# One row of low and high parts: products of 256, 272 and 264 columns, with the sample sums joined after the product

## The chip, the core and the metric

The kernel runs on one core of one Trainium2 chip. The metric is the device time of one execution in microseconds (us). Three runs of the kernel before gave 1385.54 to 1386.02 us, with a median of 1385.92 us. The core has a matrix engine (PE, with its weight loads listed as PEld), a vector engine (DVE), a scalar engine (ACT), a third elementwise engine (POOL) and a queue for transfers (SP). Each works through its own instructions in their written order and waits for the others by semaphores.

## The reference

One layer of a hybrid decoder is computed in float32, for a prompt of 256 tokens and for 8 samples of one token each. D is 2048. Cut to the products:

```
x, w_in ... : float32
xn = rms_norm(x, g_mix)
z  = xn @ w_in                       # 2048 -> 3584
u_pool, u_lru, u_gel, c_a, c_b = split(z)
y_pool = pool_mixer(u_pool) @ w_pool_br          # 512 -> 2048
y_lru  = (rg_lru(conv4(u_lru)) * gelu(u_gel)) @ w_lru_br     # 1024 -> 2048
y_conf = silu(layer_norm(conv31(c_a * sigmoid(c_b)))) @ w_conf_br
g_a, g_b, g_c = split(sigmoid(xn @ w_gate + b_gate))         # 2048 -> 6144
x = x + (g_a * y_pool + g_b * y_lru + g_c * y_conf) @ w_out
hid = square(relu(rms_norm(x, g_mlp) @ w_up))                # 2048 -> 8192
x = x + hid @ w_down                                         # 8192 -> 2048
y = rms_norm(x, g_final)
```

Both token groups go through the same weights, so the kernel puts them side by side: 256 prompt columns and 8 sample columns, N = 264 columns in all. The samples also carry small states (convolution tails, the recurrence's last value) that are read and written back.

## The kernel before

**Three products for one.** Float32 accuracy is reached with products of the type float32r. Each weight w is split into a high part `whi` (w rounded to float32r, a cast on ACT, line 190) and a low part `wlo = w - whi` (a subtraction on DVE, line 191). Each activation is split in the same way into a high and a low part. One 128x128 block of weights then takes three products into the same accumulator `acc` of 128x264: whi by high (line 207), whi by low (line 208), wlo by high (line 209). The small fourth product, wlo by low, is left out. In the first four chunks line 920 issues the same products in another order. A weight block is loaded anew for each product.

**Chunks and groups.** Weights arrive in chunks of 128x1024 values (two rows of four 128x128 blocks). A group is a stretch of 512 output columns: four accumulators, filled over 8 chunks for an inner size of 2048, 4 for 1024 and 2 for 512. There are 67 dense groups. The 8 gate blocks of the recurrence and the pooling's group map are four half-size chunks and one more. The main loop walks over the chunks; for chunk i it issues the cast and the subtraction of chunk i+3, then the products of chunk i, at the end of a group the evacuation of its four accumulators, and then background work (`run_bg`): the convolutions, the scan, the norms, given out by credits for each engine and by delays in chunks (`later`).

**What sets the order.** Every engine follows this one written order. Four buffers hold split weights (`NHI = 4`), so the cast of chunk i+3 waits for the last product of chunk i-1. There are 8 accumulators: four for the group that runs, four for the one being emptied. The two parts of an activation lie in tiles at a pitch of 320 columns, high parts first and low parts behind them: `A` (the normalised input, later the merged branches and the hidden values), `L` and `LH` (the recurrence), `Q` (pooling and Conformer branch), `xn2` (the MLP's input).

**Places that the prediction speaks of.** `branch_evac` at line 769 multiplies an accumulator of a branch by its gate on DVE; for the Conformer branch POOL adds the other branches (line 775), and one and two chunks later ACT and DVE split the sum into `A` (lines 781 and 785). `down_evac` (line 855) adds an accumulator to the residual X; in the last quarter of the MLP it is followed by a square on ACT (line 818), an addition on POOL (line 820) and a scaling on ACT (line 860). The last two chunks of the kernel are interleaved by accumulator, so that the four accumulators of the last group are done one after the other. `last_evac` (lines 849 and 850) empties the very last one in two halves. A product with `ones` (line 1013) then sums the squares, ACT takes the root (line 1020), DVE refines it (lines 1025 to 1027), and the scaled rows are sent out (lines 1036 and 1037).

Of the kernel before, what the change touches and what calls it, by code (L numbers as in the profile page):

```python
# [15 lines left out]
P = 128  # L16
D = 2048
TP = 256
TS = 8
# [27 lines left out]
PITCH = 320  # L47
# [43 lines left out]
def hybrid_step(ctx: ExitStack, tc: tile.TileContext, first, par_in, st_in, wall, y_out, st_out):  # L91
# [14 lines left out]
    a_all = cpool.tile([P, 32 * PITCH], F32R, name="A")  # L106
    b_all = [cpool.tile([P, 8 * PITCH], F32, name=f"tmp{i}", tag=f"B{i}") for i in range(4)]
    qtmp = cpool.tile([P, 16 * PITCH], F32, name="qtmp", tag="Q")
    L = cpool.tile([P, 16 * PITCH], F32R, name="L", tag="L")
# [14 lines left out]
    def operand(t, k):  # L124
        return t[:, k * PITCH:k * PITCH + N]

    def operands(t, k, n=2):
        return t[:, k * PITCH:(k + n) * PITCH].rearrange("p (k c) -> p k c", k=n)[:, :, :N]

    def A(k):  # L130
        return operand(a_all, k)

    def acc():
        return psum.tile([P, 512], F32, name="acc", tag="acc")

# [70 lines left out]
    def mm3(ps, whi_t, wlo_t, xh, xl, first, last):  # L206
        nc.tensor.matmul(ps[:, :N], whi_t, xh, start=first, stop=False)  # L207
        nc.tensor.matmul(ps[:, :N], whi_t, xl, start=False, stop=False)  # L208
        nc.tensor.matmul(ps[:, :N], wlo_t, xh, start=False, stop=last)  # L209
# [138 lines left out]
    def x_sum():  # L348
        nc.vector.tensor_tensor(sq4[:, 0:2, :], sq4[:, 0:2, :], sq4[:, 2:4, :], op=ALU.add)
        nc.vector.tensor_tensor(sq4[:, 0, :], sq4[:, 0, :], sq4[:, 1, :], op=ALU.add)  # L350
        spend(dve=1.2)
        later(1, lambda: total_fold(operand(L, 0), G[:, 10, :], sq4[:, 0, :]))

    def x_rms():
        rms_close(operand(L, 0))
        later(1, lru_x_scale)
# [44 lines left out]
    def LH(s):  # L401
        if not l_at:
            l_at.append(cpool.tile([P, 16 * PITCH], F32R, name="LH", tag="L"))
        return operands(l_at[0], s.start) if isinstance(s, slice) else operand(l_at[0], s)
# [66 lines left out]
    def lru_gate_mm(ct, c, j):  # L471
# [9 lines left out]
        nc.scalar.activation(TM[:, ct, :], out[1][:, :N], AF.Sigmoid, bias=pv("b_lru_x", ct))  # L481
# [9 lines left out]
    def lru_tail():  # L491
# [3 lines left out]
        def scratch():  # L495
            S.append(operands(cpool.tile([P, 16 * PITCH], F32, name="lscr", tag="L"), 0, 8))
# [93 lines left out]
    def conf():  # L590
# [33 lines left out]
        def mean():  # L624
            kept.append(ones_mm(Q(4)))

        def halves():
            total_fold(Q(4), CT[:, 1, :], CT[:, 0, :])
# [42 lines left out]
        stage_split(q, 2, lambda c: Q(slice(4 + 2 * c, 6 + 2 * c)), lambda c: Q(slice(12 + 2 * c, 14 + 2 * c)),  # L671
# [15 lines left out]
    def Q(s):  # L687
        if not q_at:
            q_at.append(cpool.tile([P, 16 * PITCH], F32R, name="Q", tag="Q"))
        return operands(q_at[0], s.start) if isinstance(s, slice) else operand(q_at[0], s)  # L690

    def pooling():
# [28 lines left out]
        stage_split("pool", 2, lambda c: Q(slice(2 * c, 2 * c + 2)), lambda c: Q(slice(8 + 2 * c, 10 + 2 * c)), lambda c: DU[:, 2 * c:2 * c + 2, :])  # L721
        mark("pool", "pool")

    def grp_mm(c):
        assert "pool" in done
        hi, lo = whi[:, c % NHI, :], wlo[:, c % NHI, :]
        for gi in range(4):
            s = slice(gi * P, (gi + 1) * P)
            ps = acc()
            mm3(ps, hi[:, s], lo[:, s], Q(gi), Q(8 + gi), True, True)  # L730
            nc.scalar.activation(DU[:, gi, :], ps[:, :N], AF.Copy, scale=pv("pool_scale", gi))
        stage_split("pool", 2, lambda c: Q(slice(2 * c, 2 * c + 2)), lambda c: Q(slice(8 + 2 * c, 10 + 2 * c)), lambda c: DU[:, 2 * c:2 * c + 2, :])
# [5 lines left out]
    def bpart(k):  # L738
        if not M:
            M.extend(cpool.tile([P, 8 * PITCH], F32R, name=f"xn2{i}", tag=f"B{i}") for i in range(4))  # L740
        return operand(M[k // 8], k % 8), operand(M[2 + k // 8], k % 8)
# [52 lines left out]
    def out_evac(m, ps):  # L794
# [3 lines left out]
        hi, lo = bpart(m)  # L798
# [13 lines left out]
        if m == KD - 1:  # L812
            later(4, lambda: total_fold(LH(0), G[:, 10, :], sq2))
            later(6, lambda: rms_close(LH(0)))
# [7 lines left out]
    def hid(q, k):  # L822
        if q % 2 == 0:
            return A(k), A(16 + k)
        return LH(k), Q(k)

    def up_evac(q, m, ps):
        hi, lo = hid(q, m)
# [23 lines left out]
    def down_evac(q, m, ps):  # L852
        if (q, m) == (3, KD - 1):
            return last_evac(ps)
# [10 lines left out]
    def group(gi):  # L865
        name, k0, _, m = groups[gi]
        if name == "w_in":
            def rhs(i):
                return A(i), A(16 + i)
# [3 lines left out]
        if name == "w_gate":  # L873
            return (lambda i: (A(i), A(16 + i))), (lambda c, p: gate_evac(m // 4, m % 4, c, p))
        if name == "w_pool_br":
            assert "grp" in done
            return (lambda i: (Q(i), Q(8 + i))), (lambda c, p: branch_evac(0, m, c, p))
        if name == "w_lru_br":
            assert "lru" in done
            return (lambda i: (LH(i), LH(8 + i))), (lambda c, p: branch_evac(1, m, c, p))  # L880
        if name == "w_conf_br":
            assert "conf" in done
            return (lambda i: (Q(4 + i), Q(12 + i))), (lambda c, p: branch_evac(2, m, c, p))
        if name == "w_out":
            return (lambda i: (A(i), A(16 + i))), (lambda c, p: out_evac(m * 4 + c, p))
        if name == "w_up":
            return bpart, (lambda c, p: up_evac(m // 4, (m % 4) * 4 + c, p))
        q = k0 // 16
        return (lambda i: hid(q, i)), (lambda c, p: down_evac(q, m * 4 + c, p))
# [260 lines left out]
```

## Time and profile before

| | us |
|---|---|
| three runs: median, lowest, highest | 1385.92, 1385.54, 1386.02 |
| the profiled execution | 1385.61 |
| its span, first to last instruction | 1383.8 |
| PE busy | 1373.5 |
| DVE busy | 835.4 |
| ACT busy | 721.5 |
| POOL busy | 94.4 |

The page of a profile gives each engine's busy time, its busy tenths in 40 slices of the span, the transfers, the chain of work that ended last, and the costliest groups of instructions. A row such as `L209 PE MATMUL acc<-A,wlo 128*128 128x264 f32 x1952` is a group: line, engine, operation, the tiles written and read, the shape and the count. In a timeline each row has a start, a length, and in brackets how long the engine had been idle before it and what ended that. The length of a product includes its way through the pipeline and overlaps the next product; how long a product really takes from the engine is read from the distance between two starts.

### The profile page before, as it was taken

What the parts mean: (1) busy time and instruction counts of PE and PEld (TensorE: products, weight loads), DVE (VectorE), ACT (ScalarE), POOL (GpSimd) and SP (SyncE); (2) the same over time, 40 slices, a digit from 0 to 9 for tenths busy, and PEclk for the clock granted to TensorE, in tenths of its full rate; (3) what the DMA queues carried; (4) which work ended last, traced back from release to release, by engine and by line L of the source; (5) the groups of instructions that cost most, each with busy time, mean ns of one, the idle gap of its engine ahead of it and who ended that gap; (6) DMA issues with size and microseconds to landing.
All of it is one profiled execution on the core that took longest, in us unless ns stands there. A gap on an engine that the chain in (4) does not pass through costs nothing.

```text
span 1383.8 us, 26656 instructions
## 1 busy us (share of the span) xinstructions
PE 1373.5 (99%) x11421; PEld 1371.8 (99%) x11421; DVE 835.4 (60%) x1052; ACT 721.5 (52%) x1021; POOL 94.4 (7%) x125
## 2 busy tenths in 40 slices
PE   9999999999999999999999999999999999999997
PEld 9999999999999999999999999999999999999997
DVE  8785787776766658565555455555455545455544
ACT  7757576666664645455544334543344533354544
POOL 0220010110102013010000000000000000000012
PEclk9999999999999999999999999999999999999999
DMA  8555555555565554655555555555555555555552
GB/s 331 205 177 190 187 189 189 182 185 183 183 216 181 180 184 158 209 179 178 194 182 184 183 183 184 184 184 184 182 184 184 183 184 184 184 185 182 184 182 76
DMA packets 40822, 257.49 MB, mean 186 GB/s; under 512 B 4480, under 2 KB 6784, under 8 KB 11776
## 3 DMA queue, kind: packets, MB, share of 16 engines
q1 hardware_dynamic: 40272, 255.19, 53.3%
q8 instruction: 89, 1.46, 0.4%
q10 hardware_dynamic: 432, 0.61, 0.1%
q14 instruction: 29, 0.24, 0.1%
HBM read 252.57 MB, written 3.21 MB: 185 GB/s over the span
## 4 chain that ended last, share of the span: by engine, by line
PE 99%; DVE 0%; DVEq 0%; ACT 0%; issue 0%
PE acc L209 33%; PE acc L208 33%; PE acc L207 32%; PE acc L920 1%; PE acc L301 0%; DVE y L1036 0%; DVE acc L1027 0%; DVEq L1127 0%; DVE G L1026 0%; DVE acc L1025 0%; PE acc L1013 0%; PE acc L284 0%; ACT rstd L1020 0%; DVE G L850 0%; DVE X L849 0%
## 5 line engine op out<-in xcount | busy, mean ns | idle before, releaser
L191 DVE TENSOR_TENSOR wlo<-raw,whi 128x1024 fp32r<-128x1024 f32 (+1 forms) x478 | 585.0, 1226 | 523.8 <-ACT whi L190 523.4
L190 ACT CAST whi<-raw 128x1024 fp32r<-128x1024 f32 (+1 forms) x478 | 494.7, 1038 | 595.2 <-PE acc L208 546.1
L209 PE MATMUL acc<-A,wlo 128*128 128x264 f32 x1952 | 553.1, 283 | 0.0
L208 PE MATMUL acc<-A,whi 128*128 128x264 f32 x1952 | 552.4, 283 | 0.0
L207 PE MATMUL acc<-A,whi 128*128 128x264 f32 x1952 | 546.9, 280 | 0.0
L207 PEld LDWEIGHTS acc<-A,whi 128*128 128x128 f32 x1952 | 366.8, 188 | 0.0
L209 PEld LDWEIGHTS acc<-A,wlo 128*128 128x128 f32 x1952 | 365.9, 187 | 0.0
L208 PEld LDWEIGHTS acc<-A,whi 128*128 128x128 f32 x1952 | 365.7, 187 | 0.0
L209 PE MATMUL acc<-xn,wlo 128*128 128x264 f32 x1024 | 291.7, 285 | 0.0
L207 PE MATMUL acc<-xn,whi 128*128 128x264 f32 x1024 | 289.2, 282 | 0.0
L208 PE MATMUL acc<-xn,whi 128*128 128x264 f32 x1024 | 286.0, 279 | 0.0
L208 PEld LDWEIGHTS acc<-xn,whi 128*128 128x128 f32 x1024 | 192.5, 188 | 0.0
L207 PEld LDWEIGHTS acc<-xn,whi 128*128 128x128 f32 x1024 | 192.2, 188 | 0.0
L209 PEld LDWEIGHTS acc<-xn,wlo 128*128 128x128 f32 x1024 | 191.5, 187 | 0.0
L209 PE MATMUL acc<-LH,wlo 128*128 128x264 f32 x640 | 182.1, 285 | 0.0
L208 PE MATMUL acc<-Q,whi 128*128 128x264 f32 x644 | 180.5, 280 | 0.0
L207 PE MATMUL acc<-LH,whi 128*128 128x264 f32 x640 | 180.4, 282 | 0.0
L208 PEld LDWEIGHTS acc<-Q,whi 128*128 128x128 f32 x644 | 120.9, 188 | 0.0
L207 PEld LDWEIGHTS acc<-LH,whi 128*128 128x128 f32 x640 | 120.2, 188 | 0.0
L209 PEld LDWEIGHTS acc<-LH,wlo 128*128 128x128 f32 x640 | 119.8, 187 | 0.0
L820 POOL TENSOR_TENSOR G<-G 128x264 f32<-128x264 f32 x28 | 25.7, 919 | 796.8 <-ACT G L818 795.9
L600 ACT ACTIVATE G<-tmp,par 128x256 f32<-128x256 f32 x120 | 54.2, 499 | 1.5 <-DVE G L603 0.8
(194 smaller groups left out, 791.0 us busy)
## 6 DMA issues: line engine op xcount, KB each, us to landing
raw<-wall_dram SPq DMA_DIRECT2D x226, 1024.0 KB, 4.8
raw<-wall_dram SPq DMA_DIRECT2D x12, 512.0 KB, 6.1
raw<-first_dram SPq DMA_DIRECT2D x6, 512.0 KB, 8.3
X<-first_dram SPq DMA_DIRECT2D x6, 264.0 KB, 7.8
raw<-wall_dram SPq DMA_DIRECT2D x5, 256.0 KB, 3.0
tmp<-first_dram SPq DMA_DIRECT2D x3, 388.0 KB, 4.8
y_dram<-y SPq DMA_DIRECT2D x3, 264.0 KB, 2.2
tmp<-st_dram SPq DMA_DIRECT2D x4, 188.0 KB, 5.2
```

Of the source, the lines that this page charges most:

```text
L190: nc.scalar.copy(h[:, s], r[:, s])
L191: nc.vector.tensor_tensor(lo[:, s], r[:, s], f(h[:, s]), op=ALU.subtract)
L207: nc.tensor.matmul(ps[:, :N], whi_t, xh, start=first, stop=False)
L208: nc.tensor.matmul(ps[:, :N], whi_t, xl, start=False, stop=False)
L209: nc.tensor.matmul(ps[:, :N], wlo_t, xh, start=False, stop=last)
L600: nc.scalar.activation(dst[:, ct, :TP], vext[:, ct, k:k + TP], AF.Copy, scale=par[:, w:w + 1])
L820: nc.gpsimd.tensor_tensor(sq2, sq2, t, op=ALU.add)
L920: nc.tensor.matmul(pss[m][:, :N], w[:, i % NHI, s], x, start=i == kt == k == 0, stop=False)
```

## The change

The low and the high part of an activation now lie in one row of 528 columns: 264 low columns (256 prompt, 8 sample) and then 264 high columns (256 prompt, 8 sample). The pitch is 640, and the row begins 56 columns in. The three products are cut in another way:

- whi by columns 0 to 255 of the row: the low parts of the prompt, 256 columns, into columns 8 to 263 of the accumulator
- whi by columns 256 to 527: the low parts of the samples and all high parts, 272 columns, into columns 0 to 271
- wlo by columns 264 to 527: all high parts, 264 columns, into columns 8 to 271

So the accumulator has the low part of the sample sums in columns 0 to 7, the prompt in columns 8 to 263 and the rest of the sample sums in columns 264 to 271. `join` adds the two: ACT copies columns 0 to 7 to a small tile `side`, and DVE adds that to columns 264 to 271. It runs once for each of the 288 accumulators, ahead of the evacuation, which then reads columns 8 to 271 (`tokens`). In the first triple of an accumulator the product of 272 columns goes first, since it starts the sum; elsewhere the order is 256, 272, 264. The number of products and of weight loads is unchanged.

```diff
-PITCH = 320
+PITCH = 640
+SKEW = 56
...
-    a_all = cpool.tile([P, 32 * PITCH], F32R, name="A")
-    b_all = [cpool.tile([P, 8 * PITCH], F32, name=f"tmp{i}", tag=f"B{i}") for i in range(4)]
+    a_all = cpool.tile([P, KD * PITCH], F32R, name="A")
+    b_all = [cpool.tile([P, 4 * PITCH], F32, name=f"tmp{i}", tag=f"B{i}") for i in range(4)]
...
+    def part(t, k, a, n):
+        at = k * PITCH + SKEW + a
+        return t[:, at:at + n]
...
+    def both(t, k):
+        return part(t, k, 0, 2 * N)
...
+    def tokens(ps):
+        return ps[:, TS:TS + N]
+
+    side, joined = cpool.tile([P, 4, TS], F32, name="side"), []
+
+    def join(ps):
+        t = side[:, len(joined) % 4, :]
+        joined.append(t)
+        nc.scalar.copy(t, ps[:, :TS])
+        nc.vector.tensor_tensor(ps[:, N:N + TS], ps[:, N:N + TS], t, op=ALU.add)
...
-    def mm3(ps, whi_t, wlo_t, xh, xl, first, last):
-        nc.tensor.matmul(ps[:, :N], whi_t, xh, start=first, stop=False)
-        nc.tensor.matmul(ps[:, :N], whi_t, xl, start=False, stop=False)
-        nc.tensor.matmul(ps[:, :N], wlo_t, xh, start=False, stop=last)
+    def mm(k, ps, w, x, start, stop=False):
+        a, b = ((TP, 2 * N), (0, TP), (N, 2 * N))[k]
+        o = (0, TS, TS)[k]
+        nc.tensor.matmul(ps[:, o:o + b - a], w, x[:, a:b], start=start, stop=stop, skip_group_check=True)
+
+    def mm3(ps, whi_t, wlo_t, x, first, last):
+        for k in (0, 1) if first else (1, 0):
+            mm(k, ps, whi_t, x, first and k == 0)
+        mm(2, ps, wlo_t, x, False, last)
...
-            mm3(ps, hi[:, s], lo[:, s], operand(L, ct), operand(L, 8 + ct), True, True)
+            mm3(ps, hi[:, s], lo[:, s], both(L, ct), True, True)
+            join(ps)
             out.append(ps)
-        nc.scalar.activation(RA[:, ct, :], out[0][:, :N], AF.Sigmoid, bias=pv("b_lru_a", ct))
+        nc.scalar.activation(RA[:, ct, :], tokens(out[0]), AF.Sigmoid, bias=pv("b_lru_a", ct))
...
-    def last_evac(ps):
+    def last_evac(whole):
         m = KD - 1
         for s in (slice(0, N // 2), slice(N // 2, N)):
+            if s.start:
+                join(whole)
+            ps = tokens(whole)
             x = X[:, m, s]
             nc.vector.tensor_tensor(x, x, ps[:, s], op=ALU.add)
...
                 for m in range(4):
-                    fn(m, pss[m])
+                    if (gi, m) == (len(groups) - 1, 3):
+                        last_evac(pss[m])
+                    else:
+                        join(pss[m])
+                        fn(m, tokens(pss[m]))
```

The other edits fetch the parts from their new places (`high`, `low`, `highs`, `lows` in place of `operand` and `operands`).

In the change, lines stand some 30 to 40 further down: the products are on line 237, the cast and the subtraction on 218 and 219, the copy and the addition of `join` on 161 and 162, the square and the scaling of the tail on 854 and 897, the additions of the residual on 892 and 888. On PE, in the second group of the kernel, where the last accumulator's first triple is followed by the first accumulator's second one, the change now has:

```order
L237 MATMUL acc<-A,whi 128x272
L237 MATMUL acc<-A,whi 128x256
L237 MATMUL acc<-A,wlo 128x264
L237 MATMUL acc<-A,whi 128x256
L237 MATMUL acc<-A,whi 128x272
L237 MATMUL acc<-A,wlo 128x264
```

Nothing moved on PE but the widths and, after the first triple, the order of the low and the high product.

On DVE the Conformer branch's groups of two chunks each (subtraction `wlo` of two chunks, four evacuations, four low parts of `A`) stood before as

```order
L191 TENSOR_TENSOR wlo<-raw,whi 128x1024 x2
L769 TENSOR_TENSOR G<-acc,G 128x264 x4
L785 TENSOR_TENSOR A<-G,A 128x264 x4
L191 TENSOR_TENSOR wlo<-raw,whi 128x1024 x2
L769 TENSOR_TENSOR G<-acc,G 128x264 x4
```

and stand in the change as

```order
L219 TENSOR_TENSOR wlo<-raw,whi 128x1024 x2
L162 TENSOR_TENSOR acc<-acc,side 128x8
L805 TENSOR_TENSOR G<-acc,G 128x264
L162 TENSOR_TENSOR acc<-acc,side 128x8
L805 TENSOR_TENSOR G<-acc,G 128x264
L162 TENSOR_TENSOR acc<-acc,side 128x8
L805 TENSOR_TENSOR G<-acc,G 128x264
L162 TENSOR_TENSOR acc<-acc,side 128x8
L805 TENSOR_TENSOR G<-acc,G 128x264
L821 TENSOR_TENSOR A<-G,A 128x264 x4
```

Ahead of each evacuation stands the addition of `join`, which waits for ACT's copy.

On ACT the end of the program, from the last casts of weights to the roots, was before

```order
L190 CAST whi<-raw 128x1024 x3
L990 ACT_TABLE_LOAD
L818 ACTIVATE G<-X 128x264
L860 ACTIVATE X<-X,gfin 128x264
L818 ACTIVATE G<-X 128x264
L860 ACTIVATE X<-X,gfin 128x264
L818 ACTIVATE G<-X 128x264
L860 ACTIVATE X<-X,gfin 128x264
L1020 ACTIVATE rstd<-acc,eps 128x132 x2
```

and is in the change

```order
L218 CAST whi<-raw 128x1024 x3
L1030 ACT_TABLE_LOAD
L161 COPY side<-acc 128x8 x4
L854 ACTIVATE G<-X 128x264
L897 ACTIVATE X<-X,gfin 128x264
L854 ACTIVATE G<-X 128x264
L897 ACTIVATE X<-X,gfin 128x264
L854 ACTIVATE G<-X 128x264
L897 ACTIVATE X<-X,gfin 128x264
L1060 ACTIVATE rstd<-acc,eps 128x132 x2
```

The copies for all four accumulators of the last group, the very last one among them, now stand ahead of the squares and scalings of the first three.

More of the change, by code (lines that the diff above doesn't have):

```diff
@@ L399, in hybrid_step, with LH @@
     l_at = []
[L401 removed]
+    def LH():
         if not l_at:
[L403 to L404 removed]
+            l_at.append(cpool.tile([P, 8 * PITCH], F32R, name="LH", tag="L"))
+        return l_at[0]
     def two(c):
@@ L685, in hybrid_step, with Q @@
     q_at = []
-    def Q(s):
+    def Q():
         if not q_at:
-            q_at.append(cpool.tile([P, 16 * PITCH], F32R, name="Q", tag="Q"))
-        return operands(q_at[0], s.start) if isinstance(s, slice) else operand(q_at[0], s)
+            q_at.append(cpool.tile([P, 8 * PITCH], F32R, name="Q", tag="Q"))
+        return q_at[0]
     def pooling():
```

93 lines of the change are left out of this document (49 added, 44 removed).

## The prediction

> **What bounds the kernel now.** I read the page first, for the engine that carries the span and for the chain of work that ended last.
>
> ```profile
> span 1383.8 us, 26656 instructions
> PE 1373.5 (99%) x11421; PEld 1371.8 (99%) x11421; DVE 835.4 (60%) x1052; ACT 721.5 (52%) x1021; POOL 94.4 (7%) x125
> ...
> PE   9999999999999999999999999999999999999997
> ...
> PE 99%; DVE 0%; DVEq 0%; ACT 0%; issue 0%
> ```
>
> PE is busy in every slice, and the chain is PE from end to end. Next comes the view of who waited for whom, for PE alone:
>
> ```profile
> PE acc L301 <- PEq L1121: 0.8, 1, 0.8
> PE acc L1013 <- DVE G L850: 0.3, 1, 0.3
> ```
>
> PE never waits for weights, activations or an accumulator: 0.8 us at the start and 0.3 us at the end are all. So the time is the number of products times what one product takes, and a tail. What one takes is the distance between two starts, here from the timeline of PE in the middle of the kernel and the count over most of it (the stretches of L207, of which each triple has one):
>
> ```profile
> 300.00 0.28 PE L207 MATMUL acc<-LH,whi 128*128 128x264 f32 x1
> 300.12 0.28 PE L208 MATMUL acc<-LH,whi 128*128 128x264 f32 x1
> 300.24 0.28 PE L209 MATMUL acc<-LH,wlo 128*128 128x264 f32 x1
> 300.36 0.28 PE L207 MATMUL acc<-LH,whi 128*128 128x264 f32 x1
> ...
> 20.00:1370.00 1350.00, 1053.37 (x3750) 1.00 0.53 184
> ```
>
> 3,750 triples in 1350 us are 0.3600 us a triple, 120.0 ns a product, at a granted clock of 1.00. Is that what 264 columns must cost? The first products run before PE is at speed, and the timeline from the start shows them in two cuts:
>
> ```profile
> 4.49 1.44 PE L920 MATMUL acc<-A,whi 128*128 128x264 f32 x5
> ...
> 5.51 0.86 PE L920 MATMUL acc<-A,whi 128*128 128x264 f32 x3
> ...
> 6.83 1.12 PE L920 MATMUL acc<-A,whi 128*128 128x264 f32 x8
> ```
>
> The product that starts at 5.51 is the last of the first cut, which ends at 4.49 + 1.44 = 5.93, so it lasts 0.42. Three from 5.51 last 0.86, so they start 0.22 apart: 264 columns at 1.2 columns per ns, with nothing left over. From 6.83 on the starts are 0.12 apart (eight of 0.28 in 1.12: 0.84 over seven). If the full rate is twice the starting one, 264 columns would take 110 ns. They take 120.0. So each product carries about 10 ns that its columns do not explain, 30 ns a triple, 114 us in the 3,796 triples of the program (472 dense chunks of 8 blocks, 16 gate blocks, 4 of the group map). The change can only win out of these.
>
> **Part 1: the widths.** 256 + 272 + 264 = 792 = 3 x 264. The columns, the products and the weight loads are the same in number, so a gain needs a cost that is not straight in the columns. The trace of before has only one width of this type, so the price of 256 and 272 is bounded, not read. 120.0 ns are 288 columns at 2.4 per ns, which is 9 steps of 32, or 18 steps of 16, or 264 and a fixed 24.
> - Fixed 24 columns a product: 280 + 296 + 288 = 864, no gain.
> - Steps of 16, the half step of 264 (16.5) filled up, and one step between products: 17 + 18 + 18 = 53 in place of 54 steps, 353.3 ns in place of 360.0.
> - Steps of 32: 8 + 9 + 9 = 26 in place of 27, 346.7 ns.
>
> The outer bounds are 330 ns (no excess at all) and 366.7 ns (the new place of a row in memory, 56 columns in, or of the output, 8 columns in, costs a step of 16 more). I take the middle reading, 6.67 ns a triple: it alone of the three lets a half-filled step cost something and keeps a gap between products, and the excess of 24 columns is exactly a half step and a whole one. 3,796 x 6.67 ns = **-25.3 us**.
>
> **Part 2: the joins beside the products.** Each of the 288 accumulators gets a copy of 128x8 on ACT and an addition of 128x8 on DVE. The groups by shape have near rows for both:
>
> ```profile
> L421 DVE TENSOR_TENSOR st<-acc,rstd 128x8 f32<-128x8 f32 x4 | 0.7, 164 | 0.0
> ...
> L363 ACT ACTIVATE G<-par 128x8 f32<-128x8 f32 x1 | 0.2, 203 | 0.0
> ```
>
> That is 288 x 0.20 = 58 us for ACT and 288 x 0.16 = 47 us for DVE, which takes them to 56% and 64% of the span. What hides them is the lead of the weight split, up to two chunks. It is thinnest where the Conformer branch is merged:
>
> ```profile
> 536.39 2.35 DVE L191 TENSOR_TENSOR wlo<-raw,whi 128x1024 fp32r<-128x1024 f32 x2
> 538.66 1.44 DVE L769 TENSOR_TENSOR G<-acc,G 128x264 f32<-128x264 f32 x4
> 540.02 3.06 DVE L785 TENSOR_TENSOR A<-G,A 128x264 fp32r<-128x264 f32 x4
> 543.00 2.35 DVE L191 TENSOR_TENSOR wlo<-raw,whi 128x1024 fp32r<-128x1024 f32 x2
> ...
> 549.60 2.35 DVE L191 TENSOR_TENSOR wlo<-raw,whi 128x1024 fp32r<-128x1024 f32 x2
> ...
> 551.54 0.28 PE L207 MATMUL acc<-A,whi 128*128 128x264 f32 x1
> ```
>
> Here DVE has no idle time in its brackets, and a group of two chunks keeps it 543.00 - 536.39 = 6.61 us, while PE needs 48 x 0.12 = 5.76. Each such group eats 0.85 us of the lead, and by 549.60 there is about 1 us left: the first of the two subtractions ends near 550.8, and PE comes to that chunk at 551.54. Four additions a group make it 0.66 us more, 2.6 us over the four groups, so PE should stand for 1 to 3 us here. I take 2.
>
> Elsewhere the join makes ACT stand still at a group's end. The copies come right after the group's products are issued, so ACT waits there for PE, and what stood in that chunk (four convolution products of some 0.4 us, say) and the next cast start up to a chunk later; on DVE the evacuation and the next subtraction stand behind the addition, which waits for ACT. The lead of two chunks covers this but in the crowded first 130 us, where DVE is near full. From 0 to 6 us; I take 2. Together **+4 us** (0 to 9).
>
> **Part 3: the tail.** The views of ACT, POOL, PE and DVE from the last accumulator on:
>
> ```profile
> 1372.21 0.52 ACT L860 ACTIVATE X<-X,gfin 128x264 f32<-128x264 f32 x1
> 1373.88 0.37 ACT L1020 ACTIVATE rstd<-acc,eps 128x132 f32<-128x132 f32 x1 [1.15 <-PE acc L1013]
> ...
> 1370.32 0.43 ACT L818 ACTIVATE G<-X 128x264 f32<-128x264 f32 x1 [0.46 <-DVE X L855]
> ...
> 1370.88 0.76 POOL L820 TENSOR_TENSOR G<-G 128x264 f32<-128x264 f32 x1 [0.68 <-ACT G L818]
> ...
> 1372.35 0.29 PE L209 MATMUL acc<-LH,wlo 128*128 128x264 f32 x1
> 1372.47 0.61 PE L1013 MATMUL acc<-G,ones 128*128 128x132 f32 x4
> 1373.35 1.17 PE L1013 MATMUL acc<-G,ones 128*128 128x132 f32 x8 [0.26 <-DVE G L850]
> ```
>
> Before, ACT does the squares and scalings of the last group's first three accumulators while PE is still at the next ones, and at 1372.73 it is free. In the change the copy of the very last accumulator stands ahead of them, and that waits for PE's last product, which ends at 1372.64. So ACT copies until about 1372.9, and only then come three squares and three scalings, 3 x (0.43 + 0.52) = 2.85 us. The second square ends near 1374.3, POOL adds it until 1375.1, and the product with `ones`, whose first factor is that sum, starts then or shortly after in place of 1372.47. Its six products for the first half take about 0.6 and end 0.3 later: the root starts near 1376.1 in place of 1373.88. **+2.2 us**, in bounds of 1.5 and 3. The addition between the halves of the last evacuation hides behind this.
>
> **Sum.** 1383.8 - 25.3 + 4 + 2.2 = 1364.7 us of span. The profiled execution's own time is 1385.61, 1.8 us over its span, and the median of the runs 0.3 us more: 1364.7 + 2.1 = **1367 us**, 1.4% faster. With the bounds of parts 2 and 3 alone, 1362 to 1373.
>
> **The rivals.**
> - *The excess is fixed a product, so only the additions are left: slower.* It speaks for this that all 11,250 products of the count have the same 120.0 ns whatever tile they read, and that the excess vanishes at the starting rate, as a gap between products would if it ran at its own pace beside slower columns. Against it, 120.0 ns being whole steps would be chance. The place is the whole of PE, the point from which it decides is a gain under 1.6 ns a triple (6.2 us). Time: 1385.9 + 4 + 2.2 = 1392 us. The Trainium skill speaks for it: by "TensorE: Matmul & The Clock Gate", section "Back-to-back issue gap", a warm product takes its columns at 2.4 per ns and 2.5 ns, which is straight in the columns and would leave 792 columns at the same price; that rule gives 112.5 ns for 264 columns, though, and the trace has 120.0, so something here is outside it.
> - *Steps of 32.* 3,796 x 13.3 = 50.6 us off: 1385.9 - 50.6 + 6.2 = 1341.5 us. For it: 288 is 9 steps with nothing else needed. Against it: no gap at all between products.
> - *The new places cost.* The row now starts 56 columns in, the output 8 columns in: a step of 16 more a triple and nothing won is 25.3 us: 1385.9 + 25.3 + 6.2 = 1417 us. No row of before has such a start, so nothing speaks for it but that it is new.
> - *A gain that just pays the additions*, 1 to 2.4 ns a triple: 1383 to 1388 us.
>
> **How the numbers follow.** Forecast 0.35, fixed excess 0.33, steps of 32 0.17, new places 0.08, gain paid away 0.07. Two executions of this kernel differ by well under 0.2% (2.8 us), and that is what a measurement can tell from no change. Faster by more: 0.35 + 0.17 = 0.52. Slower by more: 0.33 + 0.08 = 0.41. Within: 0.07. The range must hold both signs: from 1338, a little under the steps of 32, to 1400, the fixed excess with 9 us and 3 us of additions and some more; most of the new places and a gain well beyond 50 us are left out. The forecast's own range is 1360 to 1376.
>
> **What would show it.** In the timeline of PE: the distance behind a product of 256 columns near 113 ns and the other two at 120 (forecast), 116.7, 123.3 and 120 (fixed excess), 107 and twice 120 (steps of 32). In the view of waits: PE standing for the subtraction of line 219 near the Conformer merge, 1 to 3 us. In the tail: squares of line 854 after the last product, the root some 3.5 us behind it in place of 1.2. The forecast is wrong if a triple takes 358 ns or more, or if PE's waits add up to over 10 us.

## The result, and the profile after

| | before | changed |
|---|---|---|
| median of 14 runs each, us | 1385.41 | 1385.75 |
| lowest to highest, us | 1385.01 to 1386.02 | 1384.26 to 1387.67 |
| span of the profiled execution, us | 1383.8 | 1383.9 |

The ratio is 1.0003, with a 95% interval of 0.9995 to 1.0012: no change that can be measured. The forecast was 1367 us and faster. The page of the changed kernel, its span, its engines and its chain:

```profile
span 1383.9 us, 27199 instructions
PE 1367.4 (99%) x11421; PEld 1363.9 (99%) x11421; DVE 876.9 (63%) x1340; ACT 758.3 (55%) x1309; POOL 94.7 (7%) x125
...
PE 94%; DVE 3%; ACT 1%; POOL 1%; issue 1%; DMA 0%; DVEq 0%; ACTq 0%; POOLq 0%
```

PE is still the bound, but the chain is no longer PE alone: 6% of it now runs through DVE, ACT, POOL and issue time. The view of waits, PE alone, tells where:

```profile
PE acc L1053 <- POOL G L856: 2.7, 1, 2.7
PE acc L237 <- DVE wlo L219: 2.1, 4, 0.7
PE acc L237 <- ACT tmp L514: 1.0, 1, 1.0
PE acc L334 <- PEq L1161: 0.8, 1, 0.8
PE acc L237 <- DVE A L355: 0.5, 1, 0.5
```

Only 0.8 + 0.3 us stood here before. The products themselves did get shorter. The count of PE's products in three stretches: one with waits, one before the MLP and one in it (start and end, length, busy time and count, clock, DMA share, GB/s):

```profile
100.00:200.00 100.00, 96.96 (x799) 1.00 0.52 177
200.00:540.00 340.00, 340.00 (x2847) 1.00 0.56 189
...
700.00:1300.00 600.00, 600.00 (x5038) 1.00 0.54 184
```

A product is in the pipe for 0.28 us and the next starts 0.12 us later, so two or three of such a count were already running when the stretch began. 600 / (5038 - 2.4) is 119.15 ns a product, 357.4 ns a triple, and 340 / (2847 - 2.4) gives 358.6, against 360.0 everywhere before. The forecast had 353.3. The timeline of PE in the middle:

```profile
800.22 0.28 PE L237 MATMUL acc<-A,wlo 128*128 128x264 f32 x1
800.34 0.40 PE L237 MATMUL acc<-A,whi 128*128 128x256 f32 x2
800.58 0.28 PE L237 MATMUL acc<-A,wlo 128*128 128x264 f32 x1
800.70 0.40 PE L237 MATMUL acc<-A,whi 128*128 128x256 f32 x2
800.94 0.28 PE L237 MATMUL acc<-A,wlo 128*128 128x264 f32 x1
```

The 264 products start 0.36 apart. The trace keeps the starts in ns. From them the mean distance within a group of the MLP is 115.2 ns behind a product of 256 columns, 121.6 behind 272 and 120.1 behind 264, 356.9 together.

**The account.** PE's last product of the dense part starts at 1370.03 us in place of 1372.35. By the 60th product, with PE at speed, the changed kernel is 0.3 us late in this execution. After that, the distances over 160 ns between two starts hold 5.5 us of standing (what each is over 120 ns). So the widths gave 2.3 + 0.3 + 5.5 = 8.1 us, 2.1 ns for each of the 3,796 triples. Then 2.4 us are lost behind the last product. 0.3 - 8.1 + 5.5 + 2.4 = 0.1 us: the gain is real, and the joins take all of it back.

### The profile page after: what moved, and what is told of

Same layout as the page of the kernel before. It is cut to its first block, busy times and chain, and to the rows that moved or that the text cites. A ratio compares the mean times of both kernels' runs of the same rounds, so it can differ in the third digit from the quotient of the medians.

```text
span 1383.9 us, 27199 instructions
## 1 busy us (share of the span) xinstructions
PE 1367.4 (99%) x11421; PEld 1363.9 (99%) x11421; DVE 876.9 (63%) x1340; ACT 758.3 (55%) x1309; POOL 94.7 (7%) x125
## 4 chain that ended last, share of the span: by engine, by line
PE 94%; DVE 3%; ACT 1%; POOL 1%; issue 1%; DMA 0%; DVEq 0%; ACTq 0%; POOLq 0%
PE acc L237 93%; DVE wlo L219 1%; ACT whi L218 1%; DVE A L821 1%; POOL G L811 0%; DMA tmp<-first_dram 0%; DVE y L1076 0%; DVE G L805 0%; DVE acc L162 0%; DVE tmp L585 0%; DVE L L501 0%; ACT tmp L515 0%; ACT G L767 0%; ACT tmp L535 0%; POOL G L856 0%
## 5 line engine op out<-in xcount | busy, mean ns | idle before, releaser
L237 PE MATMUL acc<-A,whi 128*128 128x256 f32 (+1 forms) x3968 | 709.5, 282 | 1.7 <-ACT tmp L514 1.0
L237 PEld LDWEIGHTS acc<-A,whi 128*128 128x128 f32 x3968 | 608.7, 188 | 2.8 <-ACT tmp L514 1.6
L237 PE MATMUL acc<-xn,whi 128*128 128x256 f32 (+1 forms) x2048 | 366.3, 281 | 0.0
L237 PEld LDWEIGHTS acc<-xn,whi 128*128 128x128 f32 x2048 | 314.6, 188 | 0.0
L237 PE MATMUL acc<-Q,whi 128*128 128x272 f32 (+1 forms) x776 | 139.4, 281 | 0.0
L237 PE MATMUL acc<-LH,whi 128*128 128x272 f32 (+1 forms) x768 | 138.1, 282 | 0.0
L237 PE MATMUL acc<-Q,wlo 128*128 128x264 f32 x388 | 109.5, 282 | 0.0
L237 PE MATMUL acc<-LH,wlo 128*128 128x264 f32 x384 | 108.4, 282 | 0.0
L237 PEld LDWEIGHTS acc<-Q,wlo 128*128 128x128 f32 x388 | 72.9, 188 | 0.0
L237 PEld LDWEIGHTS acc<-LH,wlo 128*128 128x128 f32 x384 | 72.1, 188 | 0.0
```

Source lines behind the costliest of these rows:

```text
L237: nc.tensor.matmul(ps[:, o:o + b - a], w, x[:, a:b], start=start, stop=stop, skip_group_check=True)
```

## Experiments on the joins

**No joins.** The copy and the addition are left out, so the low part of the sample columns' sums is missing from the result.

```diff
     def join(ps):
         t = side[:, len(joined) % 4, :]
-        joined.append(t)
-        nc.scalar.copy(t, ps[:, :TS])
-        nc.vector.tensor_tensor(ps[:, N:N + TS], ps[:, N:N + TS], t, op=ALU.add)
+        return
```

> The change without the joins: the low part of the sample sums (columns 0 to 7 of each accumulator) is left out of the result. If the gain of 2.5 ns a triple is real over the whole kernel and the joins gave it back: 3796 x 2.5 ns = 9.5 us less than before, 1376 to 1378 us, with no wait of PE beyond those of before and the root 1.5 us behind the start of the last product. If the new widths themselves bring the stalls (other reasons than the join): 1381 to 1386 us.

Measured: 1378.01 us (1377.86 to 1379.53), ratio 0.9948 (0.9933 to 0.9963). PE's waits:

```profile
PE acc L332 <- PEq L1159: 0.8, 1, 0.8
PE acc L235 <- DVE A L353: 0.6, 1, 0.6
PE acc L1051 <- DVE G L887: 0.3, 1, 0.3
```

Behind the slow first 9 us no distance between two starts is over 160 ns until the end. The joins cost 1385.75 - 1378.01 = 7.7 us, 5.5 + 2.4 by the account, and 1385.41 - 1378.01 = 7.4 us is what the widths gain by themselves.

**The copy on DVE in place of ACT.**

```diff
-        nc.scalar.copy(t, ps[:, :TS])
+        nc.vector.tensor_copy(t, ps[:, :TS])
```

> The change with the copy of the join on DVE in place of ACT; nothing is left out. If it is ACT standing in the join that gives the gain back (late casts at the end of a group, squares of the tail behind the last copy): the waits of PE in the first 200 us vanish, the tail falls back to that of before, and the time is 1377 to 1380 us; DVE carries 48 us more, and the wait at the Conformer merge grows from some 0.5 us to 1 to 3 us. If the load of DVE is what makes PE wait: longer waits than in the change, 1386 to 1392 us.

Measured: 1388.14 us (1387.08 to 1389.98), ratio 1.0020 (1.0011 to 1.0030). PE's waits, all but the start's:

```profile
PE acc L237 <- DVE wlo L219: 3.6, 4, 1.2
PE acc L237 <- ACT tmp L514: 2.0, 2, 1.5
...
PE acc L237 <- DVE L L501: 0.6, 1, 0.6
PE acc L237 <- DVE A L355: 0.6, 1, 0.6
PE acc L237 <- ACT whi L218: 0.5, 2, 0.3
PE acc L1053 <- DVE G L889: 0.2, 1, 0.2
```

Two answers. The wait of line 1053 for POOL is gone (2.7 to 0.2), and the root at the end starts 1.5 us behind the start of the last product as before, so what made the tail late was ACT standing in the copy. But the standing grew from 5.5 to 10.4 us: 8.4 us in the first 200 us, and 1.6 at the Conformer merge, inside the 1 to 3 expected there. This run alone doesn't say which engine's standing hurts in the change, since DVE now stands for PE in ACT's place. The timelines of ACT, DVE and PE of the changed kernel do, at the gate blocks of the recurrence and at the pooling's group map, in order of time:

```profile
108.57 0.48 ACT L514 ACTIVATE tmp<-acc,par 128x264 f32<-128x264 f32 x1 [2.70 <-DVE acc L162]
...
125.68 0.24 ACT L161 COPY side<-acc 128x8 f32<-128x8 f32 x2
...
126.64 1.22 DVE L219 TENSOR_TENSOR wlo<-raw,whi 128x1024 fp32r<-128x1024 f32 x1
...
127.18 0.28 PE L237 MATMUL acc<-A,wlo 128*128 128x264 f32 x1
...
127.77 0.24 DVE L162 TENSOR_TENSOR acc<-acc,side 128x8 f32<-128x8 f32 x2
...
127.97 0.48 ACT L514 ACTIVATE tmp<-acc,par 128x264 f32<-128x264 f32 x1 [2.05 <-DVE acc L162]
...
128.51 0.51 PE L237 MATMUL acc<-A,whi 128*128 128x272 f32 x2 [1.04 <-ACT tmp L514]
...
189.71 0.48 ACT L767 ACTIVATE G<-acc,par 128x264 f32<-128x264 f32 x1 [1.32 <-DVE acc L162]
...
194.55 1.22 DVE L219 TENSOR_TENSOR wlo<-raw,whi 128x1024 fp32r<-128x1024 f32 x1 [1.38 <-ACT whi L218]
...
195.83 0.39 PE L237 MATMUL acc<-A,wlo 128*128 128x264 f32 x1 [0.74 <-DVE wlo L219]
```

The two copies are done at 125.92. DVE has a whole subtraction (line 219, 1.22 us) ahead of the additions, so these end at 128.01; the sigmoid of line 514 has waited 2.05 us for the first of them, and PE waits 1.04 us for the accumulator that the sigmoid reads. An addition of 0.17 us costs what is queued ahead of it on its engine. At the group map ACT again waits for the addition, 1.32 us. Then copy, addition and activation go to and fro between the two engines, 0.78 us for each of the four accumulators, where the four activations alone take 1.59 us in the next kernel. So ACT's next cast of weights starts 5.24 us behind the first of these instructions (2.52 in that kernel), DVE waits for it, and PE waits 0.74 us for the subtraction.

**The joins left out where they cost.** The recurrence's gate blocks, the group map, the Conformer branch and the last group take three products of 264 columns and no join; everything else is the change. Nothing of the computation is left out.

```diff
+    def plain(ps, whi_t, wlo_t, x, first, last):
+        for k, (w, a) in enumerate(((whi_t, N), (whi_t, 0), (wlo_t, N))):
+            nc.tensor.matmul(tokens(ps), w, x[:, a:a + N], start=first and k == 0, stop=last and k == 2)
...
-            mm3(ps, hi[:, s], lo[:, s], both(L, ct), True, True)
-            join(ps)
+            plain(ps, hi[:, s], lo[:, s], both(L, ct), True, True)
...
+    def bare(gi):
+        return gi == len(groups) - 1 or groups[gi][0] == 'w_conf_br'
...
```

> The change, but with three products of 264 columns and no join for the gate blocks of the recurrence, the group map, the Conformer branch and the very last group; nothing is left out. If the joins gave the gain back where ACT and DVE are crowded and in the tail (5.5 us of stalls of PE and 2.4 us of tail, of which the stall of 1.2 us at 194 us and those of 112 to 141 us go, too): 1378 to 1380 us. If the stalls only move to other joins of the first 200 us: 1381 to 1384. If stalls and tail were not the cause: 1385 or more.

Measured: 1377.73 us (1377.59 to 1379.80), ratio 0.9947 (0.9933 to 0.9960): 0.5% faster than the kernel before. PE's waits, and the count of the stretch in which the change stood most (799 products there):

```profile
PE acc L338 <- PEq L1165: 0.8, 1, 0.8
PE acc L237 <- DVE A L359: 0.6, 1, 0.6
PE acc L1057 <- DVE G L889: 0.3, 1, 0.3
```

```profile
100.00:200.00 100.00, 100.00 (x841) 1.00 0.56 190
```

248 of the 288 joins are still there and cost nothing that shows; the price was paid at the 40 of these four places.

## Experiments on what a product takes

These kernels change the products of 30 of the MLP's groups: every triple there but the first of an accumulator is issued with a list of widths and places, two groups to each setting. The MLP's values are then not the reference's.

```diff
+        at = chunks[i][1] - (len(groups) - 32)
+        if 0 <= at < 2 * len(SWEEP) and (c or kt):
+            x = rhs(2 * c + kt)
+            for k, (a, n, o, d) in enumerate(SWEEP[at // 2]):
...
+                nc.tensor.matmul(pss[m][:, o:o + n], w[:, i % NHI, b:b + P], x[:, a:a + n], start=False,
...
```

a is the first column of the row that is read, n the width, o the first column of the accumulator, d a shift of the weights (b is the block's first column and d, less 64 in the last block of a chunk). The times below are the distance between the starts of the first and the last of 178 products of a group, divided by 177, times three; where the two groups of a setting differ by more than half a ns, both are given, but for the MLP's first group, which has one product more. All kernels of this section but the last were executed once each.

**Widths alone**, all three from the row's first column:

> The changed kernel, but in 30 of the 32 groups of the MLP (15 pairs of neighbouring groups) all three products of a block, but for the first triple of each accumulator, are of one width and read the row from its first column: 128, 192, 240, 248, 256, 260, 264, 268, 272, 280, 288, 320, 384, 448 and 512 columns, a pair of groups each. The values of the MLP are not those of the reference, so its total time says nothing; what is read is the distance between the starts of two products in each pair of groups. Fixed excess: the distance is straight in the width, width / 2.4 + 10 ns, so 116.7 at 256, 120.0 at 264, 123.3 at 272, 143 at 320, 223 at 512. Steps of 16 and a gap of one: 113.3 at 256, 120 from 257 to 272, 126.7 from 273 to 288. Steps of 32: 106.7 at 256, 120 from 257 to 288, 133 from 289 to 320. A fourth, that the weight load is the bound: flat near 118 to 120 ns below some width and straight above it.

```
columns      128   192   240   248   256   260   264   268   272   280   288   320   512
ns, triple   335   335   336   340   340   360   360.5 380   370   387   400   440   700
ns, product  111.7 111.7 112.0 113.3 113.4 120.0 120.2 126.7 123.3 128.9 133.3 146.7 233.3
```

The counts over both groups of 256, 264, 268 and 272 columns agree to half a per cent (they hold the first triples too, which are as in the change):

```profile
812.00:855.00 43.00, 43.00 (x380) 1.00 0.57 196
...
902.00:947.00 45.00, 45.00 (x377) 1.00 0.55 187
948.00:994.00 46.00, 46.00 (x366) 1.00 0.52 174
997.00:1043.00 46.00, 46.00 (x376) 1.00 0.55 183
```

Three things fall here. Up to 240 columns a product costs 112 ns whatever its width. Above, the cost climbs unevenly: 268 columns cost more than 272, and from 256 to 260 there is a jump of 6.6 ns. The prices at 256, 260 and 264 are those that steps of 16 would give (113.3, 120 and 120), but 268, 272, 280 and 288 are not. Neither steps of 16, nor steps of 32, nor a fixed excess gives the whole row: steps would not fall from 268 to 272, and with a fixed excess 256 would save 3.3 ns and cost 116.9.

**Orders and places.**

> The same groups of the MLP, now at 264 or near it, with other places and orders; the values of the MLP are not those of the reference. Fifteen pairs of groups: three of 264 in the new row; 256, 272, 264 as in the change; 272, 256, 264; 264, 272, 256; the widths of the change with the output always from column 0; three of 264 that start 4, 8, 16, 24, 32 and 48 columns into the row; three of 256; 248, 280, 264; 240, 288, 264; 256, 288, 248. Fixed excess: 360.0 ns a triple wherever the columns sum to 792, whatever place and order, and the 357.5 in the profile of the change would have to come from elsewhere. If place in memory decides (the two whi products of the change start at another phase than before): three of 264 from the first column differ from three of 264 as before, and the start columns 4 to 48 give several values. If order decides: 256, 272, 264 gives 357.5 and 272, 256, 264 gives 360. If the place of the output decides: the output from column 0 gives another value than the change.

```
                                          ns, triple
256, 272, 264, as the change              356.8
the same, all outputs from column 0       356.9
272, 256, 264                             360.0
264, 272, 256                             360.0, 360.3
three of 264, in the change's row         365.2
three of 264 from column 4, 8, 32         360.0 to 360.3
three of 264 from column 16 | 24          364.2 | 366.6
three of 264 from column 48               370.0 and 360.0 (its two groups)
three of 256 (from 0, 256, 264)           356.5
248, 280, 264 | 240, 288, 264             364.4 | 366.6
```

Three products of 264 columns cost 360.0 to 370.0 by the column that they start from, and three of 256 cost 340.1 or 356.5. In the one pair compared, where the output goes makes no difference. The same three widths in another order make 3.2 ns.

**Moving the weights in place of the row.** Three of 264 from column 0, weights read d columns further on; then both moved; then three of 256.

> As the two sweeps before: the changed kernel with other products in 30 groups of the MLP, whose values are not those of the reference. Seven pairs of groups: three of 264 columns from the first column of the row, but the 128 weight columns read 8, 16, 24, 32, 40, 48 or 56 columns further on (64 = 256 bytes would be a full turn). Three pairs: row and weights both 16, 24 or 48 columns further on. Five pairs: three of 256 from column 8, 16, 24, 32 or 48 of the row. If the excess is a clash of the two reads of PE, the columns of the running product and the weights of the next one, it depends on the distance of the two places: moving the weights by 16, 32, 40, 48 columns gives what moving the row by 48, 32, 24, 16 gave (360 to 370, 360.0, 366.5, 364.2 ns a triple), and moving both together gives 360 as for no shift. If the place of the row alone decides: 360.0 for all seven shifts of the weights, and 364.2, 366.5, 360 to 370 for the three with both moved. If the bound at 111.7 ns is the load of weights alone, 256 from other columns keeps 113.3.

```
d                              8      16     24     32     40     48            56
264, weights moved             365.1  370.0  365.1  362.9  366.6  364.2, 360.0  360.1
264, row and weights moved            360.4  360.0                360.0, 360.5
256, row moved                 355.0  359.9  350.0  353.3         356.0
```

The counts for d = 16 and for 256 columns from column 24:

```profile
686.50:733.00 46.50, 46.50 (x380) 1.00 0.54 182
...
1196.50:1241.00 44.50, 44.50 (x382) 1.00 0.56 190
```

That is the key run. The columns streamed are the same ones as in the setting that takes 360.5, and weights from another place make it 370.0. Move both together and it is 360 again, in all six groups. And the weights moved by 40 cost what the row moved by 24 costs (366.6), by 48 what the row by 16 (364.2, in one of two groups), by 16 what the row by 48 (370.0, in one of two), by 56 what the row by 8 (360.1 and 360.0): places count by their distance, taken modulo 64 columns, which is 256 bytes. One pair of the five differs (32: 362.9 against 360.0). With the widths of the change two more pairs were run, and they agree: weights moved by 32 take 362.3, as the row moved by 32 does, and by 16 they take 366.9, beside 366.6 for the row moved by 48. So the price hangs on where the columns lie against the weights. A clash between reading the running columns and loading the next block would do that: in the trace of before the load for the product behind starts 0.01 us after the running one (800.08 and 800.07 us). This mechanism is inferred; what is shown is that the two places count together. The Trainium skill, "TensorE: Matmul & The Clock Gate", section "Step-by-step: what each phase is for", says that PE reads the streaming operand and the weights through two independent ports, so that loading the next weights takes nothing from the running product. For these float32r products the run disagrees, 360.5 against 370.0 ns.

**The whole row moved, and the change with SKEW = 0.**

> The same groups of the MLP, values not those of the reference. Eight pairs: 256, 272, 264 with the phases of the change, but the row begun 0, 8, 16, 24, 32, 40, 48 and 56 columns further on (the middle product reads from the same column as the first, not 256 columns behind it). Three pairs with all three from one phase (shift 0, 16, 32). Two with the weights 32 and 16 columns further on. Two with 272, 256, 264 at shift 16 and 32. If place decides (clash or own place), these spread over 345 to 370 ns a triple, the shift of 0 columns gives the 356.8 of the change, and one of them may be better than it. If what matters is only the order and the widths: 356.8 for all of the first eight, 360 for the last two. If 256 columns from the first column are worth 113.3 in company as they are alone, a triple from one phase gives 113.3 + 123.3 + 120.1 = 356.8.

```
row moved by (256, 272, 264)   0      8      16     24     32     40     48     56
ns, triple                     356.8  373.0  363.4  362.3  362.3  365.4  366.7  363.4
272, 256, 264                                366.7         373.0
```

```diff
-SKEW = 56
+SKEW = 0
```

> The change with the row at the first column of its pitch in place of 56 columns in; nothing is left out. By the clash of the two reads of PE at the distances swept (a row 8 columns further on in its 64 gives 373.0 ns a triple in place of 356.9): 3796 x 16 ns = 61 us more than the change, about 1445 us. If only widths and order decide: 1386 us.

Measured in the whole kernel: 1435.18 us, 49.4 over the changed kernel for a start of the row alone. SKEW = 0 is the row moved by 8 columns (56 + 8 = 64). The sweep's 16.2 ns by 3,796 triples would be 61 us. The MLP's groups do take that (373.3 ns), but up to 110 us a triple takes some 360 ns, and 373 only behind a stand of PE at 112.8 us; more on this under the order. That the place decides, and not the widths and their order alone, holds; the size was overstated.

**The low weights' product moved; three of 264 apart; the low weights moved.**

> As the sweeps before (the changed kernel, other products in 30 groups of the MLP, whose values are not those of the reference): 256, 272, 264 with the two whi products from the first column of the row, as in the change, and the wlo product from column 2, 4, 6, 10, 12, 16, 20, 24, 32, 40, 48, 56; then whi and wlo products from 4 and 12, 2 and 10, 60 and 68. If the two reads of PE clash by their distance in steps of 8 columns or more, the finer places give the value of the change (356.8 ns) up to 12, and the far ones up to 373. If the change sits at the best place by chance of one 8-column step, some of 2 to 12 are lower than 356.8, down to 350.

> The same groups, values not those of the reference: three of 264 as in the kernel before (no split of the sample columns, so no join needed), but the three places apart: the low parts 8, 16, 24, 32, 40, 48 or 56 columns behind the high parts (high and wlo product from column 0); then the wlo product that far behind the others; then the low parts 8 before the others. In the kernel before all three have one place, and 360.0 ns. If the clash depends on the places, some of these are off 360, and the lowest says what places alone would be worth without the new widths; if the new widths are needed, none is below 358.

> The change with the widths and places of the change in the last groups (256, 272, 264 columns), but the low weights wlo read from 2, 4, 6, 8, 10, 14, 16, 20, 24, 32, 40, 48, 54, 58 and 62 columns further on, two groups each (so the low weights are not those of the reference there). The columns that every product reads stay where they are. If a product is slowed where the weights of the next block and its own columns are read from the same part of the memory, then this alone changes the triple, which takes 356.8 ns as the change stands, by as much as the places of the rows did: from about 354 to 373 ns, not in steps. If only the place of the running columns and of the output counted, all fifteen settings would take 356.8 ns.

```
third product from column (change: 8)  2      4      6      10     12     20     32     56
ns, triple                             360.1  372.8  366.7  353.9  366.6  360.0  366.6  363.3, 366.7
whole row moved by 2 | 4 | 60          378.1 | 362.3, 363.3 | 360.2, 373.1
low weights moved by                   2      4      6      8      14     32     40            48     62
ns, triple                             368.9  366.5  362.7  360.0  363.3  372.8  366.7, 360.1  360.0  364.6
```

Two columns (8 bytes) can change a triple by 12 to 21 ns (356.8 to 368.9 or 378.1); for the third product alone they change it by -3 or +10. Of fifteen places of the low weights none takes less than 360.0, with the streamed columns as they are in the change: 356.8 is a lucky place, though not the best, which was 353.9 with the third product at 10. That one isn't to be had with this row, where the high part follows the low one at column 264, 8 modulo 64. Three products of 264 with the places of one product moved took 360.2 to 366.6 in all fifteen such settings: none of these places alone gives what the widths give.

**The order in the whole kernel**: 272, 256, 264 in every triple.

```diff
-        for k in (0, 1) if first else (1, 0):
+        for k in (0, 1):
```

> The change with the order of the first two products of a triple the other way: 272, 256, 264 in place of 256, 272, 264 in every triple of the kernel. In the last groups this order took 360.0 ns a triple against 356.8. If the order is worth that everywhere, 3,796 triples by 3.2 ns are 12.1 us: about 1398 us (1395 to 1400). If the order counts in the groups of the sweep alone, 1386 us.

Measured: 1415.63 us (1414.92 to 1419.17), ratio 1.0227 (1.0210 to 1.0244). The price was 30 us in place of 12. PE's count in the MLP:

```profile
700.00:1300.00 600.00, 600.00 (x4912) 1.00 0.53 181
```

600 / (4912 - 2.4) is 122.2, 366.6 ns a triple, steady in every group of the MLP, where the sweep's two groups with the same instructions kept 360.0. So one setting has more than one steady rhythm. The sweeps show it too: the third product from column 16 took 366.6 in both groups of one kernel, and 360.0 and 363.3 in another. So a difference of a few ns between two settings may be one of rhythm.

The traces show where a rhythm changes. PE in the reversed order, in three stretches and at the point between the first two:

```profile
440.00:472.00 32.00, 32.00 (x264) 1.00 0.51 169
475.00:545.00 70.00, 70.00 (x585) 1.00 0.53 181
565.00:597.00 32.00, 32.00 (x264) 1.00 0.63 226
...
473.38 0.29 PE L317 MATMUL acc<-Q,ones_r 128*128 128x264 f32 x1
```

The triple takes some 367 ns, then 360, then 367. The first change comes behind a single product with ones, put between two triples at 473.38 us, the second behind PE's wait for a subtraction at 563 us. In the kernel with SKEW = 0 the change at 112.8 us follows a stand of PE as well. So a disturbance can move PE from one rhythm to another, which then stays. Another product with ones, at 449.8 us, changed nothing, and which rhythm follows is open.

## Why the prediction was wrong

**Part 1 failed**, at the step "the excess of 24 columns is exactly a half step and a whole one", taken as steps of 16. The runs showed that the width alone doesn't set the price: a floor of 112 ns, an uneven climb, a price that moves with the place of the columns against the weights (340 to 360 ns for three of 256), and more than one rhythm. A trace of steps is there, half as large: in 116 of 203 groups of the sweeps (the first of each left out) the triple is within 0.2 ns of a multiple of 3.33 ns, where chance would give some 24; why isn't shown. The agreement of 264 columns with 288 at 2.4 per ns says nothing on 256 and 272; the prediction had rated it against the fixed excess, for which it would be chance. Its outer bounds, 330 and 366.7, did hold the measured 356.9 to 358.6. The term of -25.3 us was -8.1. The bounds it had set for itself, a triple of 358 ns and waits of 10 us, were too lax: with 360.0 - 2.1 = 357.9 ns and some 7 us neither is crossed, and two thirds of the gain are missing. The finer sign told it: 115.2, 121.6 and 120.1 ns in place of 113 and twice 120, midway between those and the 116.7, 123.3 and 120 of the fixed excess.

**The fixed excess** fell as well. Three of 256 take 340 ns in one place, and the sum over 256, 272 and 264 in the change isn't three times 264. The rule quoted from the Trainium skill for it, "TensorE: Matmul & The Clock Gate", section "Back-to-back issue gap", is straight in the columns; 380 ns at 268 and 370 at 272 are not. The same section gives that rule for an isolated product, and says that the spacing in a stream is set by the weight load as well as by the product. With that the floor of 112 ns agrees in kind, though not in figures; no run here tells what sets the floor.

**Part 2** was near in size, 5.5 us against 4 (0 to 9), and wrong about the place. At the Conformer merge, which was to cost 2, PE stands 0.6 us (one wait near 555 us). The additions made DVE's group of two chunks there longer by 0.36 us (6.97, from 547.00 to 553.97 us) and not by 0.66, since the four low parts of `A` took 2.6 us in place of 3.06. The rest lies between 112 and 196 us: 2.5 us at 112 to 130, 1.0 at 141 and 1.4 at 194. The thin lead there was known ("the crowded first 130 us, where DVE is near full"), but the mechanism put first, ACT standing for PE, isn't what decides there. In the rows shown ACT stands for DVE's addition, 1.32 to 2.70 us, because that is queued behind a subtraction. The prediction had it the other way round, the evacuation and the next subtraction waiting behind the addition.

**Part 3** was right in mechanism and near in size: 2.2 forecast, 2.4 measured. PE, ACT and POOL at the end of the changed kernel:

```profile
1370.03 0.28 PE L237 MATMUL acc<-Q,wlo 128*128 128x264 f32 x1
...
1370.67 0.17 ACT L161 COPY side<-acc 128x8 f32<-128x8 f32 x1 [1.59 <-DVE X L888]
...
1371.30 1.60 POOL L856 TENSOR_TENSOR G<-G 128x264 f32<-128x264 f32 x2 [17.19 <-ACT G L854]
...
1372.96 1.62 PE L1053 MATMUL acc<-G,ones 128*128 128x132 f32 x12 [2.65 <-POOL G L856]
1373.94 0.37 ACT L1060 ACTIVATE rstd<-acc,eps 128x132 f32<-128x132 f32 x1 [0.51 <-PE acc L1053]
```

The squares and POOL's sums start only behind the copy, and the root starts 3.6 us behind the end of the last product in place of 1.2 (forecast some 3.5). The copy itself starts 0.36 us behind that end, behind the first half's addition to X (line 888).

**What came true** is the rival given 0.07, a gain that just pays the additions: 2.1 ns a triple, inside its 1 to 2.4, and 1385.75 in its 1383 to 1388. The rival named no mechanism, so only its number came true. "Faster by 1.4%" was wrong; the range of 1338 to 1400 held the time. The new places, rated 0.08 because nothing in the trace spoke for them, turned out to be worth 49 us at SKEW = 0: it was not a small rival, it was one that happened not to apply at 56.

## What to carry to other kernels

For products that each load new weights, a price read at one width and one place is a price for that place only: try a few starts of the row against the weights, modulo 256 bytes, before building on a new width. A small operation added on an engine with spare time can cost nothing in most places and its whole queue in a few: find those in the view of waits and keep the old form there. Here 248 of 288 joins cost nothing, and leaving out the other 40 made a change of no effect into one of 0.5%. And where the bounds of a price take in both signs, the chance of the sign should be as open as the bounds.

## What was not expected of the hardware

- Narrowing a float32r product below 240 columns gains nothing where each loads new weights: 111.7 ns at 128 as at 192 columns, 112.0 at 240.
- From one place of the row, 268 columns cost more than 272, 126.7 against 123.3 ns.
- Moving only the low weights by 8 bytes changes a triple by 12 ns, moving all the columns by 8 bytes 21 ns; their distance modulo 256 bytes is what counts, but for one pair of the seven compared (in two of the others it holds for one of the two groups).
- The same instructions can settle at 360.0 or at 366.6 to 370.0 ns a triple and stay there for a whole group, in one case for all of the MLP; a single product put between, or a stand of PE of a few tenths of a us, can move them. Open: which rhythm follows, and, if two reads of PE do clash, which part of the memory they share. All sweeps were made in the MLP, with one layout of the weights.
